# Down projection of an FFN: eleven of 22 blocks with seven products, interleaved with the next block

## The chip, the cores and the metric

One core of one Trainium2 chip runs the whole kernel in one launch. The metric is device time in microseconds, and the number compared is the median of several runs. A profiled execution gives the views quoted below. Its engines are PE (TensorE, with PEld for its weight loads), DVE (VectorE), ACT (ScalarE), POOL (GpSimd) and SP (SyncE, which issues nearly all the transfers here).

## The reference, cut to what matters

A single encoder layer on 256 tokens of width 2048: an FFN, a mixer, and a second FFN.

```python
def swiglu(x, w_gate_up, w_down):
    gate, up = jnp.split(x @ w_gate_up, 2, axis=-1)
    return (jax.nn.silu(gate) * up) @ w_down
...
x = x + 0.5 * rms_norm(swiglu(rms_norm(x, pre1), w_gate_up1, w_down1), post1)
...                                          # mixer, ends in  @ w_mix_out
x = x + 0.5 * rms_norm(swiglu(rms_norm(x, pre2), w_gate_up2, w_down2), post2)
```

The matrix `w_down` is 5632 x 2048 in float32. The change lies in the product with it, which the kernel does twice, and touches the smaller product with `w_mix_out` (2048 x 2048) through the same class.

## The kernel before

**Float32 by two parts.** Every weight and every activation is split into a high part `h`, a cast to the format in which TensorE is fast (ACT, line 176), and a low part `l`, the rest (DVE, line 177). A product of two 128-row tiles is then three matmuls: high by high, high by low, low by high (`three`, line 414, with its matmul at line 420).

**Blocks.** The contraction dimension of 5632 goes in 22 blocks (`NU`) of 256 rows, and the 2048 output columns in two column runs of 1024: `Pairs.run(0)` and `run(1)`. A block of one run is a 256 x 1024 weight tile, 1 MB, brought by one transfer into one of three `raw` buffers (`load`, line 141). Left operands are the 22 `ht` tiles, 256 x 256 each, made by the gate part of the FFN. The four outputs `c[m][n]` are four banks of the accumulating memory, 128 x 512 each.

**Plain blocks.** A block has 2 x 2 x 2 products of 128 x 128 by 128 x 512: eight products, 24 matmuls. Its two halves of 1024 columns of `raw` are cast and subtracted by `split_half` (line 168) into an `h` and an `l` buffer, of which there are five each.

**Blocks with seven products.** For the blocks in `MIXED` the method `seven` (line 435) uses Strassen's scheme in Winograd's form: sums of the right-hand quarters `b11`, `b12`, `b21`, `b22` and sums of the left-hand quarters, and seven products instead of eight, 21 matmuls. On the right it splits `b11` alone, adds (line 444), splits the lower half, adds (448), splits the upper half, adds (450), and splits the new lower half, called `last`. So it takes four `h` buffers, and a plain block two. On the left, `sums_of` (line 378) has made four sums when the gate part made `ht`, and `left_sums` (line 537) splits them into a tile `sp` once per run. Four further banks `p` collect products that belong to several outputs; `fold` (line 476) adds them to `c` after the last such block, between two plain ones.

**Order.** In run 0 blocks with seven products and plain ones alternate: 1, 0, 3, 2, 5, 4 and so on to 17, 16, 18, and 19, 20, 21 at the end. `MIXED` is the nine even blocks from 0 to 16. Run 1 does the same with the blocks under 14 first, since their `ht` tiles (pool `early`) make room for the pool `post` of the end of the layer. The two last blocks of run 1 are held back (`HELD`) and used by `finish` (line 588), which writes the order of the end by hand. Everywhere else the program's order gives priorities, and a planner sets each engine's order from them, from its own costs and from the buffers that it reckons to be free.

**Memory.** `open_far` (line 193) opens a pool at the far end. In the gate part it holds `xt`, the layer's input, 32 KB per partition. In the down projection it holds `sp` (two buffers) and `pg`, the gains. The column sums of the blocks under 16 lie where the tile `X` was, that of block 16 in the pool `work`. A tile `z` with one buffer (line 805) serves as a workplace in `units` (line 836), which turns the gate's results into `ht`: from a bank directly, or, for a block in `MIXED`, through a copy in `z` from which the sums are made too (lines 858 to 866).

Of the kernel before, what the change touches and what calls it, by code (L numbers as in the profile page):

```python
# [11 lines left out]
F32 = mybir.dt.float32  # L12
F32R = mybir.dt.float32r
# [7 lines left out]
P = 128  # L21
# [16 lines left out]
def hymba_layer_kernel(  # L38
# [30 lines left out]
    hip = ctx.enter_context(tc.tile_pool(name="hip", bufs=5))  # L69
# [6 lines left out]
    def nm(s):  # L76
        uid[0] += 1
        return f"{s}_{uid[0]}"
# [308 lines left out]
    class Blocks:  # L387

        def __init__(self, tiles, sums):
            self.tiles, self.sums = tiles, sums

# [37 lines left out]
            cs = slice(n * 512, (n + 1) * 512)  # L432
            self.three(("c", m, n), a[:, k, 0, ms], a[:, k, 1, ms], hs[k][:, cs], ls[k][:, cs])

        def seven(self, u):

            raw = load(self.source(u))
            b11, b12, b21, b22 = (raw[:, i * 512 : (i + 1) * 512] for i in range(4))
            four = raw.rearrange("p (i c) -> p i c", i=4)
            h = hip.tile([P, 1024], F32R, tag="h", name=nm("h"))  # L440
            l = lop.tile([P, 1024], F32R, tag="l", name=nm("l"))
            split_act(h[:, 0:512], l[:, 0:512], b11)

            nc.vector.tensor_tensor(  # L444
                four[:, 0:2], four[:, 0::3], four[:, 1:2].to_broadcast([P, 2, 512]), ALU.add
            )
            lower = split_half(raw, 1)
            nc.vector.tensor_tensor(b22, b11, b22, ALU.add)  # L448
            upper = split_half(raw, 0)
            nc.vector.tensor_tensor(b21, b22, b21, ALU.add)  # L450
            last = split_half(raw, 1)
            if not self.p:
                self.p = [pa(), pa(), pb(), pb()]
            a, w = self.tiles[u], self.left_sums(u)

            def lhs(k, m):
                return [a[:, k, i, m * P : (m + 1) * P] for i in range(2)]

            def summed(j):
                return [w[:, j, i, :] for i in range(2)]  # L460

            def rhs(two, n):
                return [x[:, n * 512 : (n + 1) * 512] for x in two]

            for at, left, right in (
                (("p", 0), lhs(0, 0), rhs((h, l), 0)),
                (("c", 0, 0), lhs(1, 0), rhs(lower, 0)),
                (("c", 0, 1), summed(S4), rhs(lower, 1)),
                (("p", 1), summed(S1), rhs(upper, 0)),
                (("p", 3), summed(S3), rhs(upper, 1)),  # L470
                (("p", 2), summed(S2), rhs(last, 1)),
                (("c", 1, 0), lhs(1, 1), rhs(last, 0)),
            ):
                self.three(at, *left, *right)

        def fold(self):
# [12 lines left out]
            add(y22, p5, y21, ALU.subtract)  # L489
            add(c[1][1], c[1][1], y22, ALU.add)  # L490

        def work(self, upto):

            while self.pos < upto:
                u = self.order[self.pos]
                if u in self.sums:
                    self.seven(u)
                else:
                    hs, ls = split_load(self.source(u))
                    if self.pos == self.after + 1:  # L500
                        self.fold()
                    places = [(k, m, n) for k in range(2) for m in range(2) for n in range(2)]
                    if self.pos in (self.after, self.after + 1):

                        places.sort(key=lambda at: at[1:])
                    for k, m, n in places:
                        self.plain(u, hs, ls, m, n, k)
                self.pos += 1

    class Pairs(Blocks):  # L510
# [2 lines left out]


        HELD = 2

        def __init__(self, w, orders, tiles, sums, room, gain_src):

            super().__init__(tiles, sums)
            self.w, self.orders = w, orders  # L520
# [273 lines left out]
    def ffn(gated, w_dn, post_gain, again, gain=None, lead=None, aside=None):  # L794

        with ExitStack() as st:
# [7 lines left out]
            def room_for(tag):  # L804
                return work.tile([P, 512], F32, tag=tag, name=nm(tag))

            def sums_room():
                n = len(sums)
# [27 lines left out]
            def units(c, scale):  # L836
# [10 lines left out]
                for j in range(2):  # L847
                    bank = (pa, pb)[j]()
                    for i in range(2):
                        for m in range(2):  # L850
                            o = i * T + m * P
                            k = 2 * j + i
                            nc.tensor.transpose(
                                bank[:, o : o + P], zs[m][:, k * P : (k + 1) * P], ident
                            )
                    g = len(hts)
                    u = bank.rearrange("p (k t) -> p k t", k=2)
                    if g in MIXED:
                        u = room_for("z").rearrange("p (k t) -> p k t", k=2)
                        nc.scalar.copy(u.rearrange("p k t -> p (k t)"), bank)  # L860
                    pool = early if g < NU - LATE else late
                    ht = pool.tile([P, 2, 2, T], F32R, tag="ht", name=nm("ht"))
                    split_act(ht[:, :, 0, :], ht[:, :, 1, :], u)
                    hts.append(ht)
                    if g in MIXED:
                        sums[g] = sums_of(u, sums_room())
                yield

            pre_stats()
# [19 lines left out]
            plain = [u for u in range(NU) if u not in MIXED]  # L889
            mixed = list(MIXED)  # L890
            order = plain[:1] + [u for ab in zip(mixed, plain[1:]) for u in ab]
            order += [u for u in plain if u not in order]

            again_order = [u for u in order if u < NU - LATE] + [u for u in order if u >= NU - LATE]
            rows = Pairs(w_dn, [order, again_order], hts, sums, work, post_gain)
# [589 lines left out]
```

## Time and profile before

| | us |
|---|---|
| median of 3 runs | 1860.9 |
| lowest, highest | 1860.32, 1861.88 |
| profiled execution | 1860.08 |
| its span, first to last instruction | 1858.2 |

The mean granted clock of TensorE over the execution is 0.999 of full speed. In the timeline the down projection of the first FFN begins at 488.3 us (run 0) and 602 us (run 1), and that of the second at about 1618 and 1732 us.

A timeline row gives the start and the length in us, engine, line, operation, tiles written and read, shapes and count, and in brackets the idle time before and what ended it. Several operations of a kind that follow on one another are merged in one row. A row of the waits gives total us, count and the longest. A row of a group gives count, busy us, mean ns, idle us before. A row of a tile's view gives the least, median and longest duration in ns.

### The profile page before, as it was taken

The numbers are of one execution on the slowest core, as the hardware profiler recorded it, in microseconds if no ns is written. First come the engines' busy times: TensorE is split into PE (matmuls) and PEld (weight loads), VectorE is DVE, ScalarE is ACT, GpSimd is POOL, SyncE is SP. The second block draws the span as 40 slices with busy tenths as digits, with TensorE's granted clock in tenths as the row PEclk, the third lists the DMA queues.
The fourth block names the chain that finished last, engine by engine and source line by source line (L and its number), as shares of the span: only waits on it lengthen the run. The fifth ranks groups of instructions, "written<-read, shape, count | busy, mean of one in ns | idle before, by whom it ended". The sixth has DMA issues, their size and how long they took to land.

```text
span 1858.2 us, 23293 instructions
## 1 busy us (share of the span) xinstructions
PE 1842.7 (99%) x8682; PEld 1533.3 (83%) x8682; DVE 1539.6 (83%) x1932; ACT 1066.8 (57%) x1421; POOL 20.8 (1%) x39
## 2 busy tenths in 40 slices
PE   9999999999999999999999999999999999999998
PEld 6888888888887887888888887888888888887886
DVE  7978888888888888577787788888888888888887
ACT  6555555555555565577677655555554555555553
POOL 1000000000000000000000000000000000000000
PEclk9999999999999999999999999999999999999999
DMA  7665655555556465555565556565665556555464
GB/s 252 204 203 184 206 200 182 181 200 200 197 207 227 181 242 203 192 179 168 168 186 153 181 190 215 181 207 193 209 207 192 195 198 208 176 195 218 180 257 155
DMA packets 180881, 365.79 MB, mean 197 GB/s; under 512 B 9256, under 2 KB 56448, under 8 KB 180000
## 3 DMA queue, kind: packets, MB, share of 16 engines
q1 hardware_dynamic: 180416, 364.17, 56.9%
q8 instruction: 68, 1.11, 0.2%
q14 instruction: 45, 0.37, 0.1%
q0 software_dynamic: 352, 0.14, 0.0%
HBM read 360.06 MB, written 4.21 MB: 196 GB/s over the span
## 4 chain that ended last, share of the span: by engine, by line
PE 78%; DVE 14%; ACT 3%; issue 3%; DMA 1%; POOL 0%; ACTq 0%; SPq 0%; DVEq 0%; POOLq 0%
PE pa L420 30%; PE pb L420 29%; DVE l L177 8%; PE pa L299 8%; PE pa L304 4%; ACT h L176 2%; DVE raw L444 2%; DVE raw L450 1%; DVE raw L448 1%; DMA raw<-in_w_ffn_gate_up_dram 1%; DVE sp L177 1%; PE pa L354 1%; PE pa L352 1%; PE pa L353 1%; ACT xt L227 1%
## 5 line engine op out<-in xcount | busy, mean ns | idle before, releaser
L176 ACT CAST h<-raw 128x1024 fp32r<-128x1024 f32 (+1 forms) x825 | 807.5, 1009 | 669.6 <-PE pb L420 309.1
L177 DVE TENSOR_TENSOR l<-raw,h 128x1024 fp32r<-128x1024 f32 (+1 forms) x825 | 936.7, 1167 | 237.0 <-ACT h L176 203.8
L420 PE MATMUL pa<-h,xt 128*128 128x512 f32 x1248 | 431.2, 392 | 0.0
L420 PE MATMUL pb<-h,xt 128*128 128x512 f32 x1168 | 407.3, 390 | 0.0
L420 PEld LDWEIGHTS pa<-h,xt 128*128 128x128 f32 x1248 | 234.1, 188 | 48.7 <-ACT h L176 0.8
L420 PEld LDWEIGHTS pb<-h,xt 128*128 128x128 f32 x1168 | 219.2, 188 | 45.9 <-DVE xt L232 0.2
L420 PE MATMUL pa<-l,xt 128*128 128x512 f32 x624 | 243.2, 390 | 0.0
L420 PE MATMUL pb<-l,xt 128*128 128x512 f32 x584 | 227.3, 389 | 0.0
L420 PE MATMUL pa<-h,ht 128*128 128x512 f32 x560 | 193.4, 390 | 0.0
L420 PE MATMUL pb<-h,ht 128*128 128x512 f32 x488 | 171.8, 390 | 0.0
L299 PE MATMUL pa<-xt,h 128*128 128x512 f32 x672 | 164.7, 394 | 0.0
L299 PEld LDWEIGHTS pa<-xt,h 128*128 128x128 f32 x672 | 123.0, 188 | 23.6
L420 PEld LDWEIGHTS pa<-l,xt 128*128 128x128 f32 x624 | 117.2, 188 | 24.0 <-DVE l L177 0.6
L420 PEld LDWEIGHTS pb<-l,xt 128*128 128x128 f32 x584 | 109.7, 188 | 22.6
L420 PEld LDWEIGHTS pa<-h,ht 128*128 128x128 f32 x560 | 105.1, 188 | 22.4 <-DVE pa L487 0.5
L420 PE MATMUL pa<-l,ht 128*128 128x512 f32 x280 | 109.3, 390 | 0.0
L420 PEld LDWEIGHTS pb<-h,ht 128*128 128x128 f32 x488 | 91.6, 188 | 19.5 <-DVE pb L488 0.3
L444 DVE TENSOR_TENSOR raw<-raw 128x1024 f32<-128x1024 f32 x80 | 97.8, 1222 | 1.6
L420 PE MATMUL pb<-l,ht 128*128 128x512 f32 x244 | 95.0, 389 | 0.0
L304 PE MATMUL pa<-xt,l 128*128 128x256 f32 x672 | 91.5, 285 | 0.0
L304 PEld LDWEIGHTS pa<-xt,l 128*128 128x128 f32 x672 | 87.1, 191 | 3.2
L420 PEld LDWEIGHTS pa<-l,ht 128*128 128x128 f32 x280 | 52.6, 188 | 11.5 <-DVE l L177 0.7
(270 smaller groups left out, 1994.6 us busy)
## 6 DMA issues: line engine op xcount, KB each, us to landing
raw<-in_w_ffn_gate_up_dram SPq DMA_DIRECT2D x350, 512.0 KB, 4.8
raw<-in_w_ffn_down_dram SPq DMA_DIRECT2D x88, 1024.0 KB, 5.2
raw<-in_w_mix_in_dram SPq DMA_DIRECT2D x52, 1024.0 KB, 5.0
raw<-in_w_mix_out_dram SPq DMA_DIRECT2D x16, 1024.0 KB, 5.0
pg<-in_post_norm_ffn_dram SPq DMA_DIRECT2D x4, 512.0 KB, 5.7
X<-in_x_dram SPq DMA_DIRECT2D x2, 1024.0 KB, 5.9
bias<-row SPq DMA_DIRECT2D x16, 128.0 KB, 4.6
kept<-X SPq DMA_DIRECT2D x2, 1024.0 KB, 4.9
```

The lines of the kernel that those rows point to most:

```text
L176: nc.scalar.copy(hi, src)
L177: nc.vector.tensor_tensor(lo, src, hi.bitcast(F32), ALU.subtract)
L227: last["act"] = nc.scalar.mul(hi, src, g)
L299: nc.tensor.matmul(slot[f], weights(hs, kk, f), xcol(xt, k), start=(k == 0), stop=(k == KT - 1))
L304: nc.tensor.matmul(slot[f][:, 0:T], weights(ls, kk, f), xcol(xt, kh * 8 + kk, 0), start=False, stop=False,)
L352: nc.tensor.matmul(dst, xh, h[:, o : o + n], start=(k == 0), stop=False)
L353: nc.tensor.matmul(dst, xh, l[:, o : o + n], start=False, stop=False)
L354: nc.tensor.matmul(dst, xl, h[:, o : o + n], start=False, stop=(k == KT - 1))
L420: nc.tensor.matmul(self.bank(at), lhs, rhs, start=(n == 1), stop=n in (ends, self.of[at]), skip_group_check=n > ends,)
L444: nc.vector.tensor_tensor(four[:, 0:2], four[:, 0::3], four[:, 1:2].to_broadcast([P, 2, 512]), ALU.add)
L448: nc.vector.tensor_tensor(b22, b11, b22, ALU.add)
L450: nc.vector.tensor_tensor(b21, b22, b21, ALU.add)
```

## The change

- `MIXED` gains blocks 20 and 21: eleven of 22. Their sums are made in `units` of the last gate group and lie in the far pool.
- The two orders are written out. Run 0: 1, 0, 3, 2, 4, 5, 6, 8, 7, 10, 9, 12, 11, 14, 13, 16, 15, 20, 21, 17, 18, 19. Run 1: 1, 0, 2, 3, 4, 5, 6, 14, 7, 8, 9, 10, 16, 11, 12, 13, 20, 21, 15, 17, 18, 19. The pool `post` opens four blocks before the end instead of eight.
- A block with seven products that is followed by a plain one calls `begin_next` twice: after its own load, to load the plain block, and before it splits `last`, to split the plain block's first half. The plain block then splits only its second half.
- `b11` gets its own buffers `ha` and `la`, 512 wide and two each, in the far pool, and no longer takes one of the five `h` and `l` buffers.
- The split sums of blocks 0 and 2 are kept from run 0 for run 1.

```diff
+        def one_block(self):
+            return (
+                p.tile([P, 1024], F32R, tag=t, name=nm(t))[:, 0:512]
+                for p, t in ((hip, "h"), (lop, "l"))
+            )
-        def seven(self, u):
+        def seven(self, u, aside=None):
             raw = load(self.source(u))
+            if aside:
+                aside()
...
-            h = hip.tile([P, 1024], F32R, tag="h", name=nm("h"))
-            l = lop.tile([P, 1024], F32R, tag="l", name=nm("l"))
-            split_act(h[:, 0:512], l[:, 0:512], b11)
+            h, l = self.one_block()
+            split_act(h, l, b11)
...
             nc.vector.tensor_tensor(b21, b22, b21, ALU.add)
+            if aside:
+                aside()
             last = split_half(raw, 1)
...
+        def begin_next(self):
+            if len(self.ahead) == 1:
+                self.ahead.append(load(self.source(self.ahead[0])))
+            else:
+                self.ahead += split_half(self.ahead[1], 0)
...
                 if u in self.sums:
-                    self.seven(u)
+                    v = self.order[self.pos + 1]
+                    if self.AHEAD and v not in self.sums and self.pos + 1 < upto:
+                        self.ahead = [v]
+                        self.seven(u, self.begin_next)
+                    else:
+                        self.seven(u)
                 else:
-                    hs, ls = split_load(self.source(u))
+                    if self.ahead:
+                        _, raw, h, l = self.ahead
+                        self.ahead = None
+                        hs, ls = zip((h, l), split_half(raw, 1))
+                    else:
+                        hs, ls = split_load(self.source(u))
...
         def left_sums(self, u):
-            w = far["pool"].tile([P, 4, 2, P], F32R, tag="sp", name=nm("sp"))
+            if u in self.kept:
+                return self.kept[u]
+            keep = self.now == 0 and u in self.keep
+            tag = f"sp{u}" if keep else "sp"
+            w = far["pool"].tile([P, 4, 2, P], F32R, tag=tag, name=nm("sp"), bufs=1 if keep else 2)
             split_act(w[:, :, 0, :], w[:, :, 1, :], self.sums[u])
+            if keep:
+                self.kept[u] = w
             return w
+        def one_block(self):                     # in Pairs
+            return (
+                far["pool"].tile([P, 512], F32R, tag=t, name=nm(t)) for t in ("ha", "la")
+            )
...
-    MIXED = range(0, 18, 2)
+    MIXED = (*range(0, 18, 2), 20, 21)
...
+                if n > 8:
+                    return far["pool"].tile([P, 4, P], F32, tag=f"su{n}", name=nm("su"), bufs=1)
...
-            rows.work(NU - LATE)
+            rows.work(NU - 4)
```

More of the change, by code (lines that the diff above doesn't have):

```diff
@@ L387, in hymba_layer_kernel @@
     class Blocks:
+        AHEAD = False
+        ahead = None
         def __init__(self, tiles, sums):
@@ L465, in seven @@
             for at, left, right in (
-                (("p", 0), lhs(0, 0), rhs((h, l), 0)),
+                (("p", 0), lhs(0, 0), (h, l)),
                 (("c", 0, 0), lhs(1, 0), rhs(lower, 0)),
@@ L515, in hymba_layer_kernel, with __init__ @@
         HELD = 2
-        def __init__(self, w, orders, tiles, sums, room, gain_src):
+        AHEAD = True
+        def __init__(self, w, orders, tiles, sums, room, gain_src, keep=()):
             super().__init__(tiles, sums)
+            self.keep, self.kept = keep, {}
             self.w, self.orders = w, orders
@@ L805, in room_for, with sums_room @@
                 return work.tile([P, 512], F32, tag=tag, name=nm(tag))
-            def sums_room():
-                n = len(sums)
+            def sums_room(u):
+                n = MIXED.index(u)
                 if n == 0:
@@ L865, in units @@
                     if g in MIXED:
-                        sums[g] = sums_of(u, sums_room())
+                        sums[g] = sums_of(u, sums_room(g))
                 yield
@@ L888, in ffn @@
             close_far()
[L889 to L895, printed above, removed]
+            orders = [
+                [1, 0, 3, 2, 4, 5, 6, 8, 7, 10, 9, 12, 11, 14, 13, 16, 15, 20, 21, 17, 18, 19],
+                [1, 0, 2, 3, 4, 5, 6, 14, 7, 8, 9, 10, 16, 11, 12, 13, 20, 21, 15, 17, 18, 19],
+            ]
+            sums.update((u, None) for u in MIXED if u not in sums)
+            rows = Pairs(w_dn, orders, hts, sums, work, post_gain, keep=(0, 2))
             rows.half_gain(far["pool"])
```

## The prediction

> **What bounds the kernel now.** I read the page first: shares by engine, then the chain that ended last.
>
> ```profile
> PE 1842.7 (99%) x8682; PEld 1533.3 (83%) x8682; DVE 1539.6 (83%) x1932; ACT 1066.8 (57%) x1421; POOL 20.8 (1%) x39
> ...
> PE 78%; DVE 14%; ACT 3%; issue 3%; DMA 1%; POOL 0%; ACTq 0%; SPq 0%; DVEq 0%; POOLq 0%
> ```
>
> TensorE works nearly all the time, so its number of matmuls is the first term. But VectorE holds 14% of the chain, and the chain in order of time shows where: in the down projections it runs over DVE. I therefore read one pair there (a seven-product block and a plain one) in the timelines, DVE first, then ACT, and one stretch of the chain for the pace of PE.
>
> ```profile
> 526.96 5.23 DVE L177 TENSOR_TENSOR l<-raw,h 128x1024 fp32r<-128x1024 f32 x5 [1.20 <-ACT h L176]
> 532.11 1.22 DVE L444 TENSOR_TENSOR raw<-raw 128x1024 f32<-128x1024 f32 x1
> 533.24 0.69 DVE L177 TENSOR_TENSOR sp<-sums,sp 128x512 fp32r<-128x512 f32 x1
> 533.84 0.69 DVE L448 TENSOR_TENSOR raw<-raw 128x512 f32<-128x512 f32 x1
> 534.52 1.22 DVE L177 TENSOR_TENSOR l<-raw,h 128x1024 fp32r<-128x1024 f32 x1
> 535.66 0.69 DVE L450 TENSOR_TENSOR raw<-raw 128x512 f32<-128x512 f32 x1
> 537.54 5.23 DVE L177 TENSOR_TENSOR l<-raw,h 128x1024 fp32r<-128x1024 f32 x5 [1.20 <-ACT h L176]
> ```
> ```profile
> 525.87 4.42 ACT L176 CAST h<-raw 128x1024 fp32r<-128x1024 f32 x5 [1.97 <-DVE raw L450]
> ```
> ```profile
> 697.33 2.72 PE pa L420 x12
> ```
>
> The pair's period on DVE is 537.54 - 526.96 = 10.58 us. By start-to-start times a 512-wide operation takes 0.60 (533.24 to 533.84), L444 1.13, L448 0.68, and the five merged subtractions 5.15 (four of 1024, one of 512), so a 1024-wide one 1.14. DVE stands still for 1.20 once per pair: after L450 ACT casts the block's last part, and DVE has nothing else ready. Without that gap a seven costs DVE 0.60 + 1.14 + 1.13 + 0.60 + 0.68 + 1.14 + 0.60 + 1.14 = 7.03 and a plain block 2.28, together 9.31.
>
> PE takes 2.72 / 12 = 0.2267 us a matmul. A pair has 21 + 24 = 45 matmuls, 10.20 us; a seven alone 4.76. So DVE falls behind by 0.38 a pair until its lead is spent, and then PE waits (the waits of the whole execution, those of one stretch, and one of them in PE's timeline):
>
> ```profile
> ACT h L176 <- PE pb L420: 309.1, 179, 5.5
> ...
> PEld pb L420 <- DVE l L177: 5.8, 14, 0.5
> ```
> ```profile
> PEld pb L420 <- DVE l L177: 2.9, 7, 0.5
> ```
> ```profile
> 559.30 0.61 PE L420 MATMUL pb<-h,sp 128*128 128x512 f32 x2
> 559.99 0.50 PE L420 MATMUL pb<-l,sp 128*128 128x512 f32 x1
> ```
>
> Fourteen waits in the whole execution, 5.8 us as the weight loads see them; at 0.38 each they cost PE 14 x 0.38 = 5.3. I take 5. The row below them is the answer for the stretch of the first FFN's down projection, and the same row comes for the second FFN's: all fourteen lie in these two. The two PE rows are one such wait: the products stand 559.30, 559.53 and 559.99, the last 0.46 behind the one before instead of 0.23. The first row tells why ACT cannot work ahead: its longest waits are for PE to give back an h buffer.
>
> **The change, part by part.** The profiled execution took 1860.08 us (span 1858.2); the median of the runs is 1860.9, so 0.8 is added to results made from the former.
>
> *Matmuls.* Eleven blocks of 22 instead of nine take seven products. Two blocks x two column runs x two FFNs save 3 x (8 - 7) = 3 matmuls each: 24 x 0.2267 = 5.4 us off PE. This is on the path, since PE is the engine that ends each run. The Trainium skill (TensorE: Matmul & The Clock Gate, Back-to-back issue gap) gives about 131 ns for a sustained 512-wide matmul with its weight load. By that the 24 would be worth 3.1 and the median below 1857.8; the trace has 227 here, without exception in unhindered stretches, and that decides.
>
> *Vector work added.* A run's DVE work becomes 11 x 9.31 = 102.4. The fold and the gains add twelve 512-wide operations, 12 x 0.60 = 7.2: 109.6. Run 0 has besides the two ht subtractions of the last gate group, 1.2, and now the column sums of blocks 20 and 21 (medians of the tile's operations, and the copy that goes ahead of them):
>
> ```profile
> L380 DVE TENSOR_TENSOR sums<-z x16: 418/418/424, 66.1 to 1497.7; 128x256 f32<-128x256 f32 x16
> L383 DVE TENSOR_TENSOR sums<-sums,z x16: 280/281/284, 67.0 to 1498.6; 128x128 f32<-128x128 f32 x16
> L384 DVE TENSOR_TENSOR sums<-z,sums x16: 280/292/294, 68.3 to 1499.0; 128x128 f32<-128x128 f32 x16
> ```
> ```profile
> L860 ACT COPY z<-pa 128x512 f32<-128x512 f32 x18 | 10.5, 581 | 3.5 <-PE pb L853 3.5
> ```
>
> That is 2 x 0.99 = 2.0, and two copies of 0.58 on ACT: 112.8 in all. Run 1 keeps the split sums of blocks 0 and 2 and saves 2 x 0.60: 108.4. PE needs (11 x 21 + 11 x 24) x 0.2267 = 112.2. So DVE fits only if its gaps go: at the old gap of 1.2 in every seven it would need 13 more than that.
>
> *The interleaving and the freed buffers.* A pair used to take six of the five h buffers; now the lone block b11 has its own, so a pair takes five. ACT can cast the next plain block's first half between upper and last, and its 1.14 subtraction covers the 1.20 gap. I take the gap as closed in the interleaved pairs: the DVE period 9.31 gains 0.9 a pair on PE's 10.20. If the cover is gone, it is 10.58 again. Eight sevens of run 0 and six of run 1 are interleaved in this way. The loads keep their order on SP; only their moment shifts. A plain block's raw buffer comes free at the last subtraction of the pair before, about 7 us of DVE work ahead of its first cast, and a load lands in less:
>
> ```profile
> raw<-in_w_ffn_down_dram SPq DMA_DIRECT2D x88, 1024.0 KB, 5.2
> ```
>
> *Lone sevens.* Some sevens are followed by another one (2 then 4, 6 then 8, 20 then 21 in run 0; 0, 6, 10, 20 in run 1). There PE needs only 4.76 from one seven to the next, while DVE needs 1.14 + 7.03 = 8.17, or about 6.97 where the lone one's gap has already been filled with the next seven's b11 and L444, which wait for no h buffer now. I take it as filled: each such step costs 6.97 - 4.76 = 2.2 of lead, unfilled 3.4. The step that leads into a lone seven gives back 10.20 - (1.14 + 7.03 + 1.20) = 0.8.
>
> *The lead at the start.* It is the time from the end of a seven's last subtraction to the matmul that reads it.
>
> ```profile
> 493.04 1.22 DVE L177 TENSOR_TENSOR l<-raw,h 128x1024 fp32r<-128x1024 f32 x1
> 495.10 1.22 DVE L177 TENSOR_TENSOR l<-raw,h 128x1024 fp32r<-128x1024 f32 x1 [0.84 <-ACT h L176]
> ...
> 610.20 4.10 DVE L177 TENSOR_TENSOR l<-raw,h 128x1024 fp32r<-128x1024 f32 x4 [1.17 <-ACT h L176]
> ```
> ```profile
> 498.48 0.39 PE L420 MATMUL pb<-l,sp 128*128 128x512 f32 x1
> ...
> 613.56 0.39 PE L420 MATMUL pb<-l,sp 128*128 128x512 f32 x1
> ```
>
> Run 0 begins with 498.48 - (493.04 + 1.22) = 4.2, run 1 with 613.56 - (610.20 + 1.22) = 2.1. The freed buffer may add up to 2 in run 0 and 1 in run 1 (estimates: DVE there stands 0.84 and 1.17 for ACT, and a plain half's buffer is worth 12 x 0.2267 = 2.7 of PE time).
> Run 0: from block 0 to 2, 10.20 - (9.31 + 1.2 + 1.2 + 2.0) = -3.5, lead 0.7 to 2.7; block 4, -2.2, a stall of 1.5 to none; 6, +0.8; 8, -2.2, a stall of 1.4 to 0.9; four pairs give back 3.6, so 20 and 21 cause none. Together 0.9 to 2.9.
> Run 1: block 2, with kept sums, 4.76 - (1.14 + 7.03 - 0.60 - 1.20) = -1.6, lead 0.5; 4 and 6, +1.7; 14, -2.2, lead 0; 8 and 10, +1.7; 16, -2.2, a stall of 0.5; 12 and 20, +1.7; 21, -2.3, a stall of 0.6. Together 1.1, or 0.1 with the larger lead.
> Per FFN 1.0 to 4.0, taken 2.5; for both 5.0, as much as now. Two times the stall is only moved.
>
> *With one answer.* The mixer's output projection is interleaved too; none of the 14 waits lies in it, so nothing to win, and its DVE work is unchanged. The far pool's new tiles lie where xt lay; the nearest sign of what they wait for is pg, loaded 0.2 us after the gate's last product, and b11's parts are needed only a block of 24 x 0.2267 = 5.4 us later:
>
> ```profile
> 488.34 0.39 PE L420 MATMUL pa<-h,ht 128*128 128x512 f32 x1
> ```
> ```profile
> 488.53 0.34 SPq L545 DMA_DIRECT2D pg<-in_post_norm_ffn_dram  x1
> ```
>
> Zero, and up to 2 an FFN if that wait holds up the casts queued behind b11 on ACT. The fold keeps its place one block after the last seven: zero.
>
> *Sum.* 1860.1 - 5.4 - 5.0 + 5.0 = 1854.7 in the profiled execution, 1855.5 as a median; with the stalls at 2 or 8, 1852.5 to 1858.5.
>
> **Rivals.**
> *The start of run 0 (not much faster).* z has one buffer. The second transposed bank can be copied only after the first block's split and sums: from the last transposes at 494.55 on 0.58 + 0.62 + 0.69 + 0.99 + 0.58 = 3.5, to 498.0, and the second pb sum needs that bank with the second product of the row at 498.02, at 498.25.
>
> ```profile
> 494.55 0.27 PE L853 MATMUL pb<-ident,s 128*128 128x128 f32 x1
> ...
> 498.02 0.62 PE L420 MATMUL pb<-h,sp 128*128 128x512 f32 x2
> ```
> ```profile
> 496.25 0.68 DVE L177 TENSOR_TENSOR ht<-pa,ht 128x512 fp32r<-128x512 f32 x1
> 496.85 0.68 DVE L177 TENSOR_TENSOR ht<-pb,ht 128x512 fp32r<-128x512 f32 x1
> ```
> ```profile
> L176 ACT CAST ht<-z x18: 620/621/622, 64.8 to 1539.5; 128x512 fp32r<-128x512 f32 x18
> L177 DVE TENSOR_TENSOR ht<-z,ht x18: 684/686/693, 65.5 to 1540.2; 128x512 fp32r<-128x512 f32 x18
> ```
>
> Against it: the old bank was free no sooner than 496.85 + 0.68 = 497.5. For it: the old ht subtractions started 1.7 after the transposes. If that delay stays, 1.4 an FFN, 2.8 in all: 1858.3.
>
> *The lone sevens' gap stays open (slower).* Each step then costs 3.4. Run 0 loses 0.7 or 2.7 at block 4 and 2.6 at 8: 3.3 to 5.3. Run 1 loses 0.7, 1.7, 1.7 and 1.8: 5.9, or 4.9 with the larger lead. An FFN loses 8.2 to 11.2, both 16 to 22 against 5 now: 1860.1 - 5.4 + 11 to 17, as a median 1867 to 1873. It decides from the point where stalls pass 5 + 5.4 = 10.4, which is about two fifths of the lone gaps open. For it: a gap of 1.20 in every seven of the trace. Against it: in the gap ACT is idle too (1.97), so only buffers kept the next work out.
>
> *The interleaving doesn't happen (slower).* If the planner issues the plain half after last all the same, each seven keeps its gap: 11 x 1.2 = 13 of DVE work a run above 111, less a lead of 3, against 112.2: about 9 a run, 36 less the old 5 and the 5.4: 1886 as a median.
>
> *No overlap between vector operations (slower).* If each took its whole duration, a pair's six 1024-wide ones would cost 0.08 and its four others 0.09 more, 0.8 a pair, and with the fold 10 a run: 111 + 10 - 3 - 112.2, about 6 a run, 24 less 5 and 5.4: 1875. The Trainium skill (VectorE: DVE Perf Modes, The DRAIN you can't avoid) says that the next operation doesn't start until the pipe is empty. The trace disagrees where operations are ready: 533.24 to 533.84 against a duration of 0.69.
>
> **How the numbers follow.** Forecast 58%, start of run 0 13%, lone gaps 22%, no interleaving 5%, no overlap 2%. 0.2% is 3.7 us, about what a measurement of this kernel can tell: faster means below 1857.2, slower above 1864.6. The forecast's own range lies mostly below (50 of its 58 points), the start's mostly within; partly filled lone gaps lie within, the rest above. Faster 0.54, same 0.19, slower 0.27. The range leaves out the last two rivals and the wider half of the lone gaps: 1851.5 to 1868.
>
> **What the new profile would show.** 8658 matmuls; in the pairs no gap of 1.20 before last, but a plain half's subtraction between L450 and last; a DVE period that follows PE's 10.20; the few waits of PE on l near blocks 4 and 8 of run 0 and 14, 16, 21 of run 1, none elsewhere; two sp casts fewer in run 1. I am wrong if waits of PE on l exceed 10 us, or if PE waits near the first seven for a bank or for ha.

## The result, and the profile after

| | median us | lowest to highest | runs |
|---|---|---|---|
| before | 1860.80 | 1860.07 to 1864.57 | 22 |
| after | 1864.93 | 1863.26 to 1866.45 | 22 |

The changed kernel is slower by 4.1 us: ratio 1.0021, with an interval of 1.0015 to 1.0028. The forecast was 1855.5, faster. The profiled execution took 1863.41 us. From the page of after, the span, the busy times, the chain's shares by engine, and the loads of the down weights (median time from issue to landing at the end):

```profile
span 1861.4 us, 23279 instructions
...
PE 1840.7 (99%) x8658; PEld 1527.0 (82%) x8658; DVE 1576.6 (85%) x1988; ACT 1086.1 (58%) x1445; POOL 21.4 (1%) x39
...
PE 72%; DVE 17%; DMA 4%; ACT 3%; issue 3%; POOL 0%; SPq 0%; DVEq 0%; ACTq 0%; POOLq 0%
...
raw<-in_w_ffn_down_dram SPq DMA_DIRECT2D x88, 1024.0 KB, 5.4
```

The 24 matmuls are gone (8682 to 8658), but PE's share of the chain fell from 78% to 72%. VectorE took 17% instead of 14%, and transfers have 4% where they had 1%. The waits of the whole execution (total us, count, longest) say who is late:

```profile
ACT ha L176 <- DMA raw<-in_w_ffn_down_dram: 20.7, 17, 2.6
ACT h L176 <- DMA raw<-in_w_ffn_down_dram: 19.8, 13, 2.9
...
PEld pb L423 <- ACT h L176: 5.5, 9, 1.2
PEld pb L423 <- DVE l L177: 5.4, 14, 0.8
PEld pa L423 <- DVE l L177: 5.3, 11, 0.9
...
PEld pa L423 <- ACT h L176: 2.1, 4, 0.7
```

PE's weight loads wait 5.5 + 5.4 + 5.3 + 2.1 = 18.3 us for `l` and `h`. Before, the same rows, of which one is missing there, came to 7.9. ACT waits 20.7 + 19.8 = 40.5 us for loads of down weights that have not landed; before it was one row of 8.4. Both FFNs have new stalls. In the first, the time from block 0's first product to the last product of the down projection went from 224.15 to 226.86 us, although 12 x 0.2267 = 2.7 us of matmuls had left it: 5.4 of new stalls. In the second the same stretch is as long as before to within 0.1 us, so some 2.7 of new stalls ate what the matmuls saved. The whole profiled execution is longer by 3.3 with 5.4 less of matmuls, so some 8.8 of stalls are new.

VectorE's timeline of after shows both the success and the failure of the interleaving:

```profile
517.19 1.22 DVE L455 TENSOR_TENSOR raw<-raw 128x1024 f32<-128x1024 f32 x1
...
524.83 1.22 DVE L455 TENSOR_TENSOR raw<-raw 128x1024 f32<-128x1024 f32 x1
...
538.66 0.69 DVE L461 TENSOR_TENSOR raw<-raw 128x512 f32<-128x512 f32 x1
540.25 3.50 DVE L177 TENSOR_TENSOR l<-raw,h 128x1024 fp32r<-128x1024 f32 x3 [0.90 <-ACT h L176]
...
545.39 1.22 DVE L455 TENSOR_TENSOR raw<-raw 128x1024 f32<-128x1024 f32 x1
...
548.93 0.68 DVE L461 TENSOR_TENSOR raw<-raw 128x512 f32<-128x512 f32 x1
549.53 3.62 DVE L177 TENSOR_TENSOR l<-raw,h 128x1024 fp32r<-128x1024 f32 x3
...
554.81 1.22 DVE L455 TENSOR_TENSOR raw<-raw 128x1024 f32<-128x1024 f32 x1
```

From 545.39 to 554.81 is one interleaved pair: after L461 the merged row of three begins at once, with a plain half in it, and the old gap of 1.20 is gone. But at 540.25 a gap of 0.90 stands in the same place: block 8's successor 10 has done its L461, and the plain block 9, whose first half should follow, isn't cast. ACT's row there, and the chain of waits in the stretch from 505 to 560 us, tell why:

```profile
539.16 2.95 ACT L176 CAST h<-raw 128x1024 fp32r<-128x1024 f32 x3 [2.75 <-DMA raw<-in_w_ffn_down_dram]
```
```profile
by line: DVE l L177 39.6%; DMA raw<-in_w_ffn_down_dram 11.0%; issue 10.4%; DVE raw L455 10.3%; DVE sp L177 6.7%; DVE la L177 6.6%; DVE raw L461 6.4%; ACT h L176 5.8%; DVE raw L459 5.6%; ACTq L176 0.1%
...
531.86 1.15 DVE l L177
533.01 0.02 issue
533.02 6.04 DMA raw<-in_w_ffn_down_dram
539.06 0.02 issue
539.09 0.04 ACTq L176
539.12 0.04 issue
539.16 1.06 ACT h L176
```

Read upward from the last row: the cast of block 9 waited for its load; the load was issued 0.02 us after VectorE's last subtraction of block 8, which gave one of the three `raw` buffers back; it landed 6.04 later. VectorE could have gone on at 538.66 + 0.60 = 539.26, so the cast of 1.06 should have begun at 538.2, which is 5.2 after the buffer came free. The load made it 6.1. Not one piece of this stretch of the chain is PE.

In run 1 a second kind of gap stands in the same place. Block 2 comes right behind block 0 there, and the first half of its plain partner, block 3, has been split already, before block 2's L461: the two subtractions from 618.48 on are block 2's `last` and block 3's second half, as the loads show that go out right behind each of them, at 619.73 and 620.87. So nothing of block 3 is left for the place before `last`:

```profile
616.62 0.68 DVE L461 TENSOR_TENSOR raw<-raw 128x512 f32<-128x512 f32 x1
618.48 2.36 DVE L177 TENSOR_TENSOR l<-raw,h 128x1024 fp32r<-128x1024 f32 x2 [1.18 <-ACT h L176]
```

The `b11` of the next block, 4, could have filled it. But its load went out at 612.72 and landed at 617.56, when VectorE had already run out of work at 616.62 + 0.60 = 617.22. Such gaps stand at 618, 645 and 672 us (1.18, 0.57 and 0.58), each behind the second of two adjacent sevens, and three of the same size in the second FFN. The gaps that a load ends directly are three in the first FFN (540, 627 and 681 us: 0.90, 0.87 and 0.58) and none in the second.

### The profile page after: what moved, and what is told of

Read it like the earlier page. It is cut to its first block, busy times and chain, and to the rows that moved or that the text cites. A ratio compares the mean times of both kernels' runs of the same rounds, so it can differ in the third digit from the quotient of the medians.

```text
span 1861.4 us, 23279 instructions
## 1 busy us (share of the span) xinstructions
PE 1840.7 (99%) x8658; PEld 1527.0 (82%) x8658; DVE 1576.6 (85%) x1988; ACT 1086.1 (58%) x1445; POOL 21.4 (1%) x39
## 4 chain that ended last, share of the span: by engine, by line
PE 72%; DVE 17%; DMA 4%; ACT 3%; issue 3%; POOL 0%; SPq 0%; DVEq 0%; ACTq 0%; POOLq 0%
PE pa L423 28%; PE pb L423 26%; DVE l L177 9%; PE pa L299 8%; PE pa L304 4%; DMA raw<-in_w_ffn_down_dram 2%; DVE raw L455 2%; ACT h L176 2%; DVE raw L459 1%; DVE raw L461 1%; DVE la L177 1%; DMA raw<-in_w_ffn_gate_up_dram 1%; PE pa L354 1%; PE pa L352 1%; PE pa L353 1%
## 5 line engine op out<-in xcount | busy, mean ns | idle before, releaser
L176 ACT CAST h<-raw 128x1024 fp32r<-128x1024 f32 (+1 forms) x793 | 795.0, 1028 | 616.2 <-PE pb L423 316.7
L177 DVE TENSOR_TENSOR l<-raw,h 128x1024 fp32r<-128x1024 f32 (+1 forms) x793 | 925.9, 1192 | 202.3 <-ACT h L176 168.8
L423 PE MATMUL pa<-h,ht 128*128 128x512 f32 x440 | 156.1, 390 | 0.4 <-ACT h L176 0.4
L423 PE MATMUL pb<-h,ht 128*128 128x512 f32 x440 | 155.0, 390 | 0.2
L455 DVE TENSOR_TENSOR raw<-raw 128x1024 f32<-128x1024 f32 x88 | 107.5, 1222 | 1.6
L423 PEld LDWEIGHTS pa<-h,ht 128*128 128x128 f32 x440 | 82.4, 188 | 18.7 <-ACT h L176 1.3
L423 PEld LDWEIGHTS pb<-h,ht 128*128 128x128 f32 x440 | 82.6, 188 | 17.9 <-DVE pb L501 1.0
L423 PE MATMUL pa<-l,ht 128*128 128x512 f32 x220 | 86.2, 392 | 1.5 <-DVE l L177 1.5
L423 PE MATMUL pb<-l,ht 128*128 128x512 f32 x220 | 86.0, 391 | 0.1
L423 PE MATMUL pb<-h,sp 128*128 128x512 f32 x192 | 70.1, 395 | 2.3 <-ACT h L176 2.3
```

Of the source, the lines that this page charges most:

```text
L176: nc.scalar.copy(hi, src)
L177: nc.vector.tensor_tensor(lo, src, hi.bitcast(F32), ALU.subtract)
L423: nc.tensor.matmul(self.bank(at), lhs, rhs, start=(n == 1), stop=n in (ends, self.of[at]), skip_group_check=n > ends,)
L455: nc.vector.tensor_tensor(four[:, 0:2], four[:, 0::3], four[:, 1:2].to_broadcast([P, 2, 512]), ALU.add)
```

## The experiments

Each was run in a series with the kernel before, on the same chip. The four series used three chips, and the median of the kernel before was 1860.48 to 1860.82 in them, so a difference between runs of two series is uncertain by some 0.3 us more. Edits are against the changed kernel unless said otherwise. "Adjacent sevens" are two blocks with seven products without a plain one between them; after has three in run 0 and four in run 1 of each FFN.

| | median us | ratio to before, interval | adjacent sevens per FFN |
|---|---|---|---|
| nine, interleaved | 1855.26 | 0.9974 (0.9964 to 0.9985) | 0 |
| nine, in turn | 1858.28 | 0.9987 (0.9978 to 0.9996) | 0 |
| ten | 1853.65 | 0.9963 (0.9950 to 0.9975) | 3 |
| ten, other order | 1860.98 | 0.9999 (0.9990 to 1.0007) | 5 |
| eleven (after) | 1864.93 | 1.0021 (1.0015 to 1.0028) | 7 |

**Nine blocks, interleaved.** The two new blocks, the written orders, the kept sums and the later `post` are undone; the interleaving and the buffers of `b11` stay.

```diff
-    MIXED = (*range(0, 18, 2), 20, 21)
+    MIXED = range(0, 18, 2)
...
-            orders = [                       # as written out
+            orders = [order, again_order]    # as before
...
-            rows.work(NU - 4)
+            rows.work(NU - LATE)
```

> Nine blocks in the old orders, nothing kept, but interleaved and with b11 in buffers of its own: the interleaving alone. Theory (VectorE is full): DVE has about 9 x 7.0 + 13 x 2.3 + 8 = 101 us of work a run against 113.6 of PE, so PE's waits on l and h fall from 5 us to under 2: 1856 to 1858. Rival (late loads): each interleaved pair holds two of the three raw buffers, ACT's waits for the loads of the down projection rise from 8 us to 40 as in the changed kernel, and PE waits as long as before or longer: 1860.8 or more. Rival (two sevens in succession): none stand so here, so 1856 to 1858 as well.

1855.26 us, 5.2 better than before, with before's number of matmuls. PE's weight loads wait 1.1 + 0.8 + 0.6 = 2.5 for `l` and `h`. So the interleaving takes away the old stalls, and all that after loses comes with the two blocks, their orders, the kept sums and the later `post`.

**Nine in turn.** The same with the interleaving off (`AHEAD = False`), so that only `b11`'s own buffers are left of the change.

> Nine blocks in the old orders with b11 in buffers of its own, but no interleaving: the freed buffers alone. If the planner fills the gap from the freed buffers without being told: 1855 to 1857, as with begin_next. If the order of the program keeps last ahead of the plain half, the gap of 1.2 stays and with it PE's waits of 5 us: 1860 to 1862.

1858.28: of the 5.2, the freed buffers bring 2.2 and the interleaving 3.0.

**Eleven in turn.** After with `AHEAD = False`.

> The changed kernel without begin_next: eleven blocks, b11's own buffers, no interleaving. Theory (VectorE is full): where the gap of 1.2 in each seven comes back, up to 11 x 1.2 a run are added to a full engine, 1875 to 1886; if the planner fills the gaps by itself from the freed buffers, near 1865. Rival (late loads): the interleaving is what makes loads late, so without it PE waits less: below 1863.

1883.7 us, ratio 1.0128 (1.0114 to 1.0142). The prediction's rival without interleaving had 1886. The weight loads wait 15.7 + 14.9 for `h`. At eleven blocks the interleaving is worth 19 us, and it did work in after.

**The split of the left sums on POOL.** This takes 0.60 off VectorE in each seven.

```diff
-            split_act(w[:, :, 0, :], w[:, :, 1, :], self.sums[u])
+            hi = w[:, :, 0, :]
+            nc.scalar.copy(hi, self.sums[u])
+            nc.gpsimd.tensor_tensor(w[:, :, 1, :], self.sums[u], hi.bitcast(F32), ALU.subtract)
```

> The changed kernel with the subtraction of the left sums' split on POOL instead of DVE (also in the mixer's output projection). Theory (VectorE is full): DVE is relieved of 0.6 us in 40 sevens of the FFNs, 24 us in all, ten per run 0; PE's waits on l and h, about 18 us as the weight loads see them, fall under 8: 1855 to 1859. Rival (late loads): no change, 1864 to 1866. Rival (two sevens in succession): each of the seven such steps of an FFN costs 0.6 less, 1860 to 1862. If POOL's operation holds up DVE's while it runs, no gain or a loss.

1893.06, 1.0175 (1.0161 to 1.0189): much slower. Groups of this kernel (count, busy us, mean ns, idle before):

```profile
L455 DVE TENSOR_TENSOR raw<-raw 128x1024 f32<-128x1024 f32 x88 | 118.4, 1345 | 2.0
L459 DVE TENSOR_TENSOR raw<-raw 128x512 f32<-128x512 f32 x88 | 75.9, 863 | 1.7
...
L577 POOL TENSOR_TENSOR sp<-sums,sp 128x512 fp32r<-128x512 f32 x28 | 51.4, 1843 | 1139.4 <-ACT sp L576 1124.3 <-DVE la L177 15.1
L577 POOL TENSOR_TENSOR sp<-su,sp 128x512 fp32r<-128x512 f32 x12 | 30.1, 2511 | 85.4 <-ACT sp L576 79.0 <-DVE la L177 6.4
```

In after L455 has a mean of 1222 and L459 of 687. VectorE lost 44 subtractions and yet was busy for 1595.1 us instead of 1576.6. Besides, the granted clock of TensorE fell to 0.50 in six stretches of this run, 27.3 us together, which after's down projections don't have; some of the 28 us lost is that. So this run didn't lessen VectorE's work, and says nothing for or against the theory that it is too much; the next but one does.

**The last pair together.** `rows.work(NU - 3)` instead of `NU - 4`, so that block 21 and block 15 are interleaved in run 1.

> The changed kernel with the pool post opened one block later, so that run 1's last seven (21) is interleaved with block 15. Theory (VectorE is full): its gap of 1.17 before last closes, and the wait of PE at that place, 1.6 us in each FFN (at 696 and 1827 in the changed kernel's profile), goes for the most part: 1861 to 1863. Rival (late loads): a load more comes late, no gain: 1865 or more.

1863.97, 1.0020 (1.0011 to 1.0029): 1 us at most. The wait near 696 us only moved on to the fold, near 704.

**One split for all.** Every seven uses block 0's split sums; the splits of the others are left out, so this kernel doesn't compute the layer.

```diff
-            if u in self.kept:
-                return self.kept[u]
+            if self.keep and self.kept:
+                return self.kept[0]
```

> The changed kernel, but in each FFN all blocks with seven products use the split left sums of block 0, so those of the others are neither cast nor subtracted (a part of the computation is replaced): 38 vector operations of 0.60 fewer, 23 us, without another engine in their place. Theory (VectorE is full, it is the amount of its work): PE's waits fall from about 13 us to under 3, 1851 to 1854. Rival (two sevens in succession, it is the places): such a step still needs 1.14 + 7.03 - 1.20 - 0.60 = 6.4 of DVE against 4.76 of PE, 1.6 instead of 2.2 short, waits near 9: 1860 to 1862. Rival (late loads): no change, 1864.

1859.78, 0.9998 (0.9989 to 1.0007). VectorE's busy time falls by 20.6 to 1556.0 us, and the kernel gains 5.1. ACT still waits 24.2 + 22.7 for the down loads, once for 5.6.

**The lone sevens spread.** Orders alone, with as many adjacent sevens as after but placed later: run 0 with 6, 8 and 14, 16 and 20, 21; run 1 with 4, 6 and 14, 8 and 10, 16 and 12, 20.

> The changed kernel with other orders: in run 0 the lone sevens are 6, 14, 20 instead of 2, 6, 20, in run 1 they are 4, 14, 10, 12 instead of 0, 6, 10, 20. The work of each engine is the same. Theory (amount of VectorE's work): 1863 to 1866. Rival (the places of the lone sevens): the lead has grown before each of them in run 0, its waits near blocks 4 and 8 (1.6 us at 526 to 531) go, and others don't come: 1860 to 1862.

1863.9 (1861.38 to 1867.22), 1.0018 (1.0009 to 1.0027). In these two pairs of orders, where the adjacent sevens stand doesn't matter.

**Ten.** Block 21 goes back to eight products, and the orders pair nearly every seven with a plain block.

```diff
-    MIXED = (*range(0, 18, 2), 20, 21)
+    MIXED = (*range(0, 18, 2), 20)
...
+                [1, 0, 3, 2, 5, 4, 7, 6, 9, 8, 11, 10, 13, 12, 15, 14, 16, 17, 20, 18, 19, 21],
+                [1, 0, 3, 2, 5, 4, 7, 14, 6, 9, 8, 11, 10, 13, 16, 12, 15, 20, 17, 18, 19, 21],
...
-            rows = Pairs(w_dn, orders, hts, sums, work, post_gain, keep=(0, 2))
+            rows = Pairs(w_dn, orders, hts, sums, work, post_gain)
...
-            rows.work(NU - 4)
+            rows.work(NU - 3)
```

> Ten blocks (0 to 16 even, and 20), interleaved, nothing kept, one lone seven in run 0 (14) and two in run 1 (4 and 10... as ordered 4 is followed by 7, the lone ones are 14 and 16 by their partners), the last seven interleaved in both. PE does 12 matmuls more than in the changed kernel, 2.7 us, and 12 fewer than with nine. Theory (amount of VectorE's work): a run asks DVE for about 107 us against 112.9 of PE, so that PE hardly waits: 1852 to 1855, faster than with nine. Rival (each block beyond nine costs what the two cost together, half each): 1859 to 1861.

1853.65 us: the fastest of all runs, faster than both kernels (before by 6.9, after by 11.3). Its VectorE is busy for 1562.1, more than in the run before last (1556.0), and it is 6.1 faster. So the amount of vector work alone isn't what after lacks.

**Ten, other order.** The same ten with after's orders, block 21 put last. The line `rows.work(NU - 4)` stays as in after, so `post` opens one block earlier than in ten; in after that step was worth 1 us at most (the last pair together).

```diff
+                [1, 0, 3, 2, 4, 5, 6, 8, 7, 10, 9, 12, 11, 14, 13, 16, 15, 20, 17, 18, 19, 21],
+                [1, 0, 2, 3, 4, 5, 6, 14, 7, 8, 9, 10, 16, 11, 12, 13, 20, 15, 17, 18, 19, 21],
```

> Ten blocks, the same work on every engine as with the ten of the kernel before this one (1853.65), with other orders: two lone sevens early in run 0 (2 and 6, as in the changed kernel) instead of one late, three in run 1 (0, 6, 10) instead of two. Theory (the places where two sevens stand together): each such step asks 7 to 8 us of DVE against 4.76 of PE, PE waits near blocks 4 and 8 of run 0 and 14 and 16 of run 1, 2 to 3 us an FFN more than with the other order: 1857 to 1860. Rival (amount of VectorE's work): the amount is the same, 1853 to 1855. Rival (late loads): the loads are as many, 1853 to 1855, or more spread.

1860.98: 7.3 slower than ten, with the same matmuls and 1559.5 us of vector work against 1562.1. The chain by line from 620 to 715 us, of ten and of this one:

```profile
by line: PE pa L423 53.2%; PE pb L423 47.2%
```
```profile
by line: PE pa L423 38.0%; PE pb L423 32.7%; DVE l L177 12.0%; DMA raw<-in_w_ffn_down_dram 6.5%; ACT h L176 3.3%; issue 2.8%; DVE raw L455 2.5%; DVE raw L461 1.4%; DVE raw L459 1.4%; DVE la L177 1.3%; DVE sp L177 0.6%; ACTq L176 0.1%
```

So the order, apart from that 1 us, puts VectorE and a load into the chain. What an adjacent pair spends is a lead, and my reading was that the lead has to be held somewhere. The next runs gave it room: a fourth `raw` buffer.

**A fourth raw buffer, on the kernel with one split.** Every fourth load of a down block goes to a buffer in the far pool.

```diff
-        raw = rawp.tile([P, 2048], F32, tag="raw", name=nm("raw"))
+        pool, how = rawp, {}
+        if src.shape[1:] == (2, 1024) and far.get("room"):     # in the down projection
+            turn_of[0] += 1
+            if turn_of[0] % 4 == 0:
+                pool, how = far["pool"], {"bufs": 1}
+        raw = pool.tile([P, 2048], F32, tag="raw", name=nm("raw"), **how)
...
```

> The kernel with one split of the left sums for all blocks (1859.8; a part of the computation is replaced), and every fourth weight block of the down projection lands in a fourth raw buffer, in the room that the other split sums leave. Theory (places): loads are not what PE waits for, 1859 to 1860. Rival (late loads): ACT's waits for the loads of the down projection (47 us there) fall under 15, and PE's waits with them: 1855 to 1857.

1854.5, 0.9967 (0.9954 to 0.9979): 5.3 better than with three buffers. The time is the one that the rival of late loads named, but its first sign is not there: ACT's waits for the loads were to fall under 15, and they went from 24.2 + 22.7 to 44.8 + 5.4 us. What fell are the waits of PE's weight loads for `l` and `h`, from 12.6 to 5.4.

**Half loads.** After with each 1 MB load of a down block as two of 512 KB, so that the first half can be cast sooner.

> The changed kernel with each load of a down projection block (and of the mixer's output projection) issued as two of 512 KB, so that b11 is there before the whole block. Theory (places): 1863 to 1865. Rival (late loads): b11's cast starts about 2 us earlier where it waited, PE's waits that lead back to a load (near 540 and 673) go: 1860 to 1862.

1863.49, 1.0015 (1.0007 to 1.0024): 1.4 better at the most.

**Ten with half loads.**

> The ten blocks with the loads in two halves: a candidate for the fastest. PE hardly waits with ten (0.4 us in the first FFN), so no theory gives more than 1 us: 1853 to 1854; slower if the doubled number of transfers delays others.

1866.76, 1.0029 (1.0019 to 1.0039): 13 worse than ten. ACT's waits for the halves rose from 6.3 + 16.5 to 62.1 + 24.1 us, though a half lands in 5.3 us, about as a whole did. Why isn't settled.

**Control: no sums kept.** After with `keep` empty, since the far pool has no room for kept sums and a fourth buffer together.

> The changed kernel without the kept split sums of blocks 0 and 2: four more casts and subtractions of 0.60 on DVE in all, 2.4 us, at the two first sevens of run 1. It is the control for the next kernel. Theories alike: 1865 to 1867.

1864.83, 1.0022 (1.0013 to 1.0031): as after. The kept sums are worth nothing that shows.

**A fourth raw buffer with eleven.** The control plus the fourth buffer.

> As the one before, eleven blocks and nothing kept, with every fourth weight block of the down projection in a fourth raw buffer, in the room of the kept sums. Theory (where two sevens stand together DVE needs a lead, and three raw buffers don't hold it): PE's waits fall by half or more, 1857 to 1860, so that eleven is about as fast as the kernel before. Rival (the places alone, DVE being too slow at them): 1864 to 1867. Rival (amount of VectorE's work): 1864 to 1867.

1855.37, 0.9970 (0.9960 to 0.9981): 9.5 less than the control with the same products, the same orders and the same vector work (1575.2 against 1578.3 us). The waits of the control and then of this one:

```profile
ACT h L176 <- DMA raw<-in_w_ffn_down_dram: 21.2, 14, 3.6
...
ACT ha L176 <- DMA raw<-in_w_ffn_down_dram: 16.2, 16, 1.9
...
PEld pb L423 <- DVE l L177: 6.4, 20, 0.8
...
PEld pb L423 <- ACT h L176: 6.1, 10, 1.7
PEld pa L423 <- DVE l L177: 4.9, 8, 0.9
...
PEld pa L423 <- ACT h L176: 2.1, 4, 0.7
```
```profile
ACT ha L183 <- DMA raw<-in_w_ffn_down_dram: 23.8, 16, 4.0
...
ACT h L183 <- DMA raw<-in_w_ffn_down_dram: 7.2, 3, 2.8
...
PEld pa L430 <- ACT h L183: 2.4, 6, 0.4
PEld pb L430 <- DVE l L184: 2.2, 6, 0.5
PEld pa L430 <- DVE l L184: 1.5, 4, 0.7
```

With `PEld pb L430 <- ACT h L183` (1.3) PE's weight loads wait 7.4 instead of 19.5 us. ACT still waits 31 us for loads, which shows how to read such a row: a wait of an engine that is ahead costs nothing. Its VectorE at the place of the gap, and the chain from 505 to 560:

```profile
538.30 1.22 DVE L184 TENSOR_TENSOR l<-raw,h 128x1024 fp32r<-128x1024 f32 x1
539.44 0.69 DVE L468 TENSOR_TENSOR raw<-raw 128x512 f32<-128x512 f32 x1
540.04 1.22 DVE L184 TENSOR_TENSOR l<-raw,h 128x1024 fp32r<-128x1024 f32 x1
```
```profile
by line: PE pa L430 55.2%; PE pb L430 45.3%; issue 0.1%
```

L468 is after's L461: the next subtraction starts 0.60 later, not 1.59, and in this stretch PE is all of the chain, where in after it was none. The three gaps of run 1 are gone too. With the fourth buffer the load of block 4 goes out at 601.41, not 612.72, and its `la` stands where the gap of 1.18 was:

```profile
615.17 0.69 DVE L468 TENSOR_TENSOR raw<-raw 128x512 f32<-128x512 f32 x1
615.77 0.69 DVE L184 TENSOR_TENSOR la<-raw,ha 128x512 fp32r<-128x512 f32 x1
616.37 0.69 DVE L184 TENSOR_TENSOR sp<-sums,sp 128x512 fp32r<-128x512 f32 x1
```

So the buffer works in two ways that these runs don't separate: a load comes sooner, and the planner, which reckons with that, puts the operations in another order.

**A fourth raw buffer with ten, in both orders.**

> Ten blocks in the order with late lone sevens (1853.65), with the fourth raw buffer. PE waits there for less than 1 us in an FFN, so no theory gives much: 1852.5 to 1854.

> Ten blocks in the order with the early lone sevens (1860.98), with the fourth raw buffer. Theory (lead held in raw buffers): most of the 7 us that this order costs goes, 1854 to 1857. Rival (the places alone): 1860 to 1861.

1855.63 in ten's order (0.9972, 0.9962 to 0.9983) and 1855.97 in the other (0.9972, 0.9961 to 0.9984). The four pairs side by side, medians in us:

| | three raw buffers | four | difference |
|---|---|---|---|
| eleven, no sums kept | 1864.83 | 1855.37 | -9.5 |
| eleven, one split | 1859.78 | 1854.50 | -5.3 |
| ten, other order | 1860.98 | 1855.97 | -5.0 |
| ten | 1853.65 | 1855.63 | +2.0 |

With three buffers the order is worth 7.3 and the split sums 5.1; with four, 0.3 and 0.9. So most of what order and vector work cost, they cost by way of the loads. (The order's 0.3 is low because ten itself is slower with four; against ten with three buffers it is 2.3.) Where nearly every seven has its plain block, the fourth buffer has little to save, and the time is 2.0 longer, though this compares two series. PE's timeline agrees: the steps beyond 0.23 between its products in the down projections add up to 0.4 us in each FFN of ten and to 1.0 and 1.6 with the fourth buffer, 1.5 of it in two waits near 682 and 1810 us. The chain before these waits runs over VectorE, not over a load; why isn't settled. The median landing doesn't explain the gains: it is 5.8 us with the fourth buffer and eleven, 5.5 in the control. The load starts sooner; it isn't quicker.

## Why the prediction was wrong, and where it was right

**Matmuls: right in number.** 24 fewer, and the unhindered pace is still 0.227 a matmul in after's timeline, so the 5.4 us were there to be had.

**Interleaving: right in the main.** The pair's period on VectorE is 554.81 - 545.39 = 9.42 (9.31 forecast). At nine blocks interleaving and buffers bring 5.2; without interleaving eleven takes 1883.7 against the 1886 of that rival. But "I take the gap as closed in the interleaved pairs" fails for three of the six of run 1 (blocks 2, 14 and 16): behind an adjacent seven the plain half goes early, and a gap of 1.18, 0.57 and 0.58 is open before `last`, 2.3 us an FFN that the sum had at nothing. Run 0 has one of 0.57 behind 20 and 21, near 587 us, which the fourth buffer doesn't close.

**Lone sevens filled: right for the lone ones.** From 517.19 to 524.83 VectorE takes 7.64 for one, with two splits of left sums in it; less one of 0.60 that is 7.04, against 6.97 filled and 8.17 open. The rival of the open gap named a time a little above the one that came (1867 to 1873), but its mechanism, the gap of the lone seven, isn't there; the gaps of run 1 are those of the seven behind it.

**No overlap: fell.** 548.93 to 549.53 is 0.60 for an operation of 0.68, now as before, against the rule of the Trainium skill (VectorE: DVE Perf Modes, The DRAIN you can't avoid) that the rival drew on. The same section says too that a next operation that isn't held starts earlier, which the prediction didn't weigh; the trace fits that sentence.

**The start of run 0: fell.** PE loses about 0.4 us there, as the steps above 0.23 between its products show, not 1.4. The far pool's tiles delayed nothing that shows.

**The loads: the step that failed.** "A plain block's raw buffer comes free at the last subtraction of the pair before, about 7 us of DVE work ahead of its first cast, and a load lands in less": they were taken at zero. The moment was right, the two times were not. About 7 us is a seven's work on VectorE; from the free buffer (533.02) to the moment at which VectorE was due for the plain half (539.26) there were 6.2, and the cast in front of it takes 1.06. That left 5.2 us, not 7, and the load took 6.0, not the median of 5.2: 0.9 late instead of 1.8 early. The median also hides that the new order frees buffers in quick succession: 26 of after's 88 down loads go out within 1.3 us of the one before and land after 6.4 to 8.0; the kernel before has no load so close behind another. Loads decide the gaps of run 1 as well: with its plain half used early, a pair needs the `b11` of the next block in the gap, and that load hadn't landed (617.56 against 617.22 at block 2). Behind an adjacent pair of sevens VectorE has little lead, so a late load can reach PE, and once VectorE is late, it also gives its buffer back late, so that the next load starts late too.

**The stalls: hence wrong by about 9.** "5.0, as much as now" came out as some 5.0 + 8.8 = 14: at the weight loads, 18.3 for 7.9. In PE's timeline the steps beyond 0.23 add up to 7.6 in the first FFN, where 1.0 to 4.0 were forecast, and 5.0 in the second; before, they were 2.4 in each. That is 7.8 of the 8.8; where the rest lies wasn't traced. Their places were partly forecast: at block 8 in run 0 (1.6) and 21 in run 1 (1.6). New are those behind a late load, near 541 (0.8) and between 671 and 683 us (0.5), and one near 645 us (1.2), where a gap of run 1 stands. So the loads that end a wait directly are the smaller part of the loss; that the rest hangs on the loads too is shown by the fourth buffer, not by these places. The sign by which I would be wrong, waits of PE on `l` above 10 us, is there: 5.4 + 5.3 = 10.7. With the fourth buffer they are 3.7, the weight loads wait 7.4, about as before, PE's steps are 1.7 and 2.2, where 2.5 an FFN was taken, and the time is 1855.37, where 1855.5 was forecast. So the other terms of the sum held together, and the loads were the term of 9.5.

Why the fourth buffer makes eleven (1855.37) no better than ten (1853.65), which has 12 more matmuls, is told in the main by PE's steps: 1.7 and 2.2 us an FFN against 0.4 and 0.4, which is more than the 2.7 of the matmuls. What stays open: why the fourth buffer adds waits with ten, why half loads harm ten, and how much of the 9.5 is the earlier load and how much the planner's other order. A fourth buffer together with kept sums wasn't tried, as the memory doesn't hold both.

## What to carry to other kernels

When a change makes one engine's work denser, work out the lead of every buffer anew: from the instruction that frees it in the new order to the moment at which the next load's first cast is due, against the landing time that the trace shows. A lead of an engine is held in buffers, and in this kernel blocks of unequal cost needed either an order that alternates them or one buffer more: the order was worth 7.3 us with ten blocks, and a fourth buffer 9.5 with eleven. The version to keep is ten blocks, nearly every one followed by a plain one: 1853.65 us.

## What the runs showed of the hardware

A subtraction of 128 x 512 on POOL took 1.84 to 2.51 us beside a busy VectorE, and VectorE's own operations became longer: 1222 to 1345 ns at 1024 wide, and 687 to 863 for L459, though L461 only from 688 to 702. I had not expected that taking work from VectorE would make it busier.

In eleven in turn, a stall of PE of 2 us was followed by a stretch of slower matmuls. Its timeline, and two windows, with the granted clock behind the busy times (0.50 and 1.00):

```profile
676.22 0.39 PE L423 MATMUL pb<-h,sp 128*128 128x512 f32 x1
678.21 0.50 PE L423 MATMUL pb<-h,sp 128*128 128x512 f32 x1 [1.60 <-ACT h L176]
...
681.61 0.63 PE L423 MATMUL pa<-l,ht 128*128 128x512 f32 x1
682.04 0.63 PE L423 MATMUL pa<-h,ht 128*128 128x512 f32 x1
```
```profile
680.30:683.30 3.00, 3.00 (x8) 2.31 (x7) 3.00 (x4) 1.74 (x3) 0.00 (x0) 0.50 0.91 322
685.00:690.00 5.00, 5.00 (x24) 4.13 (x23) 3.81 (x6) 3.03 (x4) 0.00 (x0) 1.00 0.77 319
```

The products stand 0.43 apart instead of 0.23 for about 3 us. The kernel with the split on POOL has six such stretches, of 3.4 or 6.8 us, each soon after two products that stand 1.7 to 2.4 apart. But in eleven in turn three other stalls, with products 2.0 apart (near 590, 1732 and 1819 us), are followed by a clock of 1.00, so these runs give no length from which on the clock falls. The stalls of after are shorter (1.2 at most), and behind them the pace stays.
